# Batched matrix product in float16: all stores behind the loads, two groups' outputs in the input buffers

## Chip, core and metric

One core of a Trainium2 chip runs the whole problem. The metric is the device time of one execution in microseconds; of the kernel before, 4 runs are shown, with a median of 134.69 us (134.59 to 134.77). Engines are named as the profile names them: PE (matrix engine), DVE (vector engine), ACT (scalar engine), SP (here it only issues transfers).

## What is computed

For 32 batches, a 256 x 512 matrix times a 512 x 384 matrix, all float32 in memory:

```python
# x: (32, 256, 512), y: (32, 512, 384), out: (32, 256, 384)
return np.einsum('bij,bjk->bik', x, y).astype(np.float32)
```

Inputs are 16.78 MB of x and 25.17 MB of y, the output is 12.58 MB: 54.5 MB pass between memory and the core.

## The kernel before

The 32 batches are cut into 8 groups of 4 (N = 8, Q = 4). Each group takes a slot of 32 partitions for each of its 4 batches, so that four matrix products run in four row strips of PE side by side. What is done to a group n is written in the code as steps of one letter and the group's number, and the string PLAN fixes the order in which the steps are given out:

- x n (line 87) and y n (line 96): the loads, 2.10 MB and 3.15 MB, issued on SP. There are two buffers for x and two for y. A load waits until the group that used its buffer two groups earlier has been read by DVE.
- T n: DVE rounds x to float16 (line 106, one instruction of 128 x 4096) and transposes it in 32 x 32 blocks (line 113).
- R n: DVE rounds y to float16 in four parts (line 119).
- M n (line 132): 128 matmuls of 32 rows by 384 columns. The 8 banks of PSUM are named (e, g), e for the half of the output rows (0, 1) and g for the batch (0 to 3). PE first does the 64 matmuls of e = 0, with the depth index outside and g inside, so that all four banks of the half are filled at the same time and finish together; then the 64 of e = 1.
- C n and D n (line 153): the copies from PSUM to the output tile, C on ACT and D on DVE. There is one set of 8 banks, so the matmuls of the next group into a bank wait for the copies out of it.
- S n (line 160): the store of the group, 1.57 MB, issued on SP.

All steps are held in this order on each engine's own queue. SP is a queue like the others: a store or load that waits holds back what SP issues after it. Transfers are spread over 16 DMA engines.

WIDE_GROUPS (6 before) chooses between two layouts of the output. In a group below it, a copy takes 32 partitions of a bank (4 copies a bank); the bank (1, 3) is copied by DVE (4 copies) and the other 7 by ACT (28 copies); a partition of the output tile holds 8 output rows of one batch, stored as one run of 12 KB. In a group from it on, a copy takes 64 partitions (2 copies a bank) and a partition holds two runs of 6 KB. In group 6 before, ACT copies all 8 banks (16 copies); in group 7, ACT has the banks with even g and DVE those with odd g (8 copies each).

The output tiles come from a pool of 5 buffers: the output of group 5 takes the buffer of group 0's, and so on, and its first copy waits until the earlier store has landed.

The PLAN before:

```python
PLAN = """
x0 x1 y0
T0 x2 y1
T1 R0 M0 C0 x3 y2
T2 D0 R1 M1 C1 x4 y3
T3 D1 R2 M2 C2 x5 y4
T4 D2 R3 M3 C3 x6 y5
T5 D3 R4 M4 C4 x7 S0 S1 S2 y6
T6 D4 R5 M5 C5 y7
T7 D5 R6 M6 C6 R7 M7 C7 D7 S3 S4 S5 S6 S7
"""
```

Of the kernel before, what the change touches and what calls it, by code (L numbers as in the profile page):

```python
# [1 line left out]

# [4 lines left out]


MM_DT = mybir.dt.float16
F32 = mybir.dt.float32  # L10
P = 128


Q = 4
STEP = 4
O_BUFS = 5
WIDE_GROUPS = 6

# [5 lines that stand above are left out]
T2 D0 R1 M1 C1 x4 y3  # L26
T3 D1 R2 M2 C2 x5 y4
T4 D2 R3 M3 C3 x6 y5
T5 D3 R4 M4 C4 x7 S0 S1 S2 y6
T6 D4 R5 M5 C5 y7  # L30
T7 D5 R6 M6 C6 R7 M7 C7 D7 S3 S4 S5 S6 S7
"""


@with_exitstack
def kernel(
    ctx: ExitStack,
    tc: tile.TileContext,
    x: bass.AP,
    y: bass.AP,  # L40
    out: bass.AP,
):
    nc = tc.nc

    B, I, J = x.shape
    _, _, K = y.shape

    PQ = P // Q
    R = I // PQ
    T = J // PQ  # L50
    TW = T // 2
    NE = I // P
    N = B // Q

    x_pool = ctx.enter_context(tc.tile_pool(name="x_pool", bufs=2))
    y_pool = ctx.enter_context(tc.tile_pool(name="y_pool", bufs=2))
    xr_pool = ctx.enter_context(tc.tile_pool(name="xr_pool", bufs=1))
    xt_pool = ctx.enter_context(tc.tile_pool(name="xt_pool", bufs=3))
    yr_pool = ctx.enter_context(tc.tile_pool(name="yr_pool", bufs=2))
    o_pool = ctx.enter_context(tc.tile_pool(name="o_pool", bufs=O_BUFS))  # L60
    psum_pool = ctx.enter_context(
        tc.tile_pool(name="psum", bufs=1, space=bass.MemoryType.PSUM)
    )

    keep = tc.keep_in_program_order

    bank = {
        (e, g): psum_pool.tile([P, K], F32, name=f"o_ps_{e}_{g}") for e in range(NE) for g in range(Q)
    }

    x_of, y_of, xt_of, yr_of, ps_of, o_of = {}, {}, {}, {}, {}, {}

    def width(n):
        return PQ if n < WIDE_GROUPS else 2 * PQ

    def on_vector(n, e, g):
        if n < WIDE_GROUPS:  # L80
            return (e, g) == (NE - 1, Q - 1)
        return n == N - 1 and g % 2 == 1

    def load_x(n):
        x_of[n] = x_pool.tile([P, R, J], F32, name="x_sb")
        keep(
            nc.sync.dma_start(
                out=x_of[n],
                in_=x[n * Q : (n + 1) * Q].rearrange("g (p r) j -> (g p) r j", r=R),
            )  # L90
        )

    def load_y(n):
        y_of[n] = y_pool.tile([P, T, K], F32, name="y_sb")
        keep(
            nc.sync.dma_start(
                out=y_of[n],
                in_=y[n * Q : (n + 1) * Q].rearrange("g (q t) k -> (g q) t k", t=T),
            )
        )  # L100

    def transpose_x(n):


        x_r = xr_pool.tile([P, R, J], MM_DT, name="x_r")
        keep(nc.vector.tensor_copy(x_r, x_of.pop(n)))  # L106
        xt_of[n] = xt_pool.tile([P, NE, TW, P], F32, name="xt_sb")
        b = width(n) // PQ
        src = x_r.bitcast(F32).rearrange("p (b h e) (q t) -> p b e t h q", b=b, e=NE, t=TW)
        dst = xt_of[n].rearrange("p e t (h s b) -> p b e t h s", s=PQ, b=b)  # L110
        for e in range(NE):
            for c in range(b):
                keep(nc.vector.transpose(dst[:, c, e], src[:, c, e]))  # L113

    def round_y(n):
        y_sb = y_of.pop(n)
        yr_of[n] = yr_pool.tile([P, T, K], MM_DT, name="y_r")
        for a in range(0, T, STEP):
            keep(nc.vector.tensor_copy(yr_of[n][:, a : a + STEP], y_sb[:, a : a + STEP]))  # L119

    def multiply(n):
        xt = xt_of.pop(n).bitcast(MM_DT).rearrange("p e t (m c) -> p e t m c", c=2)
        y_r = yr_of.pop(n)
        o_of[n] = o_pool.tile([P, R, K], F32, name="o_sb")
        for e in range(NE):
            for g in range(Q):
                ps_of[n, e, g] = bank[e, g]
            for t in range(T):
                for g in range(Q):
                    s = slice(g * PQ, (g + 1) * PQ)  # L130
                    keep(
                        nc.tensor.matmul(  # L132
                            ps_of[n, e, g],
                            xt[s, e, t // 2, :, t % 2],
                            y_r[s, t],
                            start=(t == 0),
                            stop=(t == T - 1),
                        )
                    )

    def collect(n, vector):
        w = width(n)
        per = P // w
        copy = nc.vector.tensor_copy if vector else nc.scalar.copy
        o = o_of[n].rearrange("p (u f) k -> p u f k", u=Q // per)
        for e in range(NE):
            for g in range(Q):
                if on_vector(n, e, g) != vector:
                    continue
                ps = ps_of.pop((n, e, g))  # L150
                a = g % per * w
                for h in range(per):
                    keep(copy(o[a : a + w, g // per, h * NE + e], ps[h * w : (h + 1) * w]))  # L153

    def store(n):
        w = width(n)
        per = P // w
        dst = out[n * Q : (n + 1) * Q].rearrange("(u g) (s f) k -> (g s) u f k", g=per, s=w)
        keep(
            nc.sync.dma_start(  # L160
                out=dst, in_=o_of.pop(n).rearrange("p (u f) k -> p u f k", u=Q // per)
            )
        )

    parts = {
        "x": load_x,
        "y": load_y,
        "T": transpose_x,
        "R": round_y,
        "M": multiply,  # L170
        "C": lambda n: collect(n, False),
        "D": lambda n: collect(n, True),
        "S": store,
    }
    for step in PLAN.split():
        parts[step[0]](int(step[1:]))


# [1 line left out]
_INS = ['x', 'y']  # L180
_OUTS = [((32, 256, 384), 'float32')]


# [23 lines left out]
```

## Time and profile before

| what | value |
|---|---|
| median of 4 runs | 134.69 us |
| profiled execution: device time | 135.1 us |
| its span, first to last instruction | 133.2 us |
| read and written | 41.94 MB, 12.58 MB |
| mean rate over the span | 410 GB/s |
| share of the span in which packets of the transfers' queue are under way | 96.9% of 16 engines |
| busy: DVE, ACT, PE | 96.0, 91.7, 58.3 us |

Times of instructions are microseconds from the start of the span. In a row of the timeline the columns are start, duration from the first to the last instruction of the run, engine, line, operation, output<-input with the form, the count, and in brackets the idle time of the engine just before with what ended it. "SPq" is the queue that issues transfers. The lines by tenths show the span in 40 slices of 3.33 us. PEclk is the share of the full clock that PE was granted.

### The profile page before, as it was taken

How to read it: one execution, taken by the hardware profiler on the slowest of the kernel's cores; microseconds unless marked ns; L12 is line 12 of the kernel's file. 1: busy time of each engine (PE TensorE's matmuls, PEld its weight loads, DVE VectorE, ACT ScalarE, POOL GpSimd, SP SyncE). 2: the span in 40 equal slices, each digit the busy share in tenths (PEclk: the TensorE clock that was granted, in tenths of full speed). 3: DMA queues.
4: the chain of work that ended last, by engine and by line, in shares of the span. 5: the costliest groups of instructions: out<-in, count | busy, mean ns of one | idle time of the engine just before them, and what ended most of it. 6: DMA issues, size and time to landing. Idle time of an engine off the chain costs nothing.

```text
span 133.2 us, 2437 instructions
## 1 busy us (share of the span) xinstructions
PE 58.3 (44%) x1024; PEld 32.7 (25%) x1024; DVE 96.0 (72%) x92; ACT 91.7 (69%) x193; POOL 0.2 (0%) x4
## 2 busy tenths in 40 slices
PE   0000003991396139623953295419540079676000
PEld 0000002560144014411531153205320045344000
DVE  0039999699969999999996999599951090766300
ACT  3000000079999999999999999999999975997200
POOL 0000000000000000000000000000000000000000
PEclk9999999999779986998699959995999559999955
DMA  5999999999999999999999999999999999999992
GB/s 118 408 443 445 428 416 438 455 421 408 443 440 435 398 450 408 428 423 448 435 401 440 421 460 389 412 424 432 450 407 450 435 413 376 433 424 415 413 417 116
DMA packets 3723, 54.68 MB, mean 410 GB/s; under 512 B 384, under 2 KB 384, under 8 KB 896
## 3 DMA queue, kind: packets, MB, share of 16 engines
q1 hardware_dynamic: 3712, 54.53, 96.9%
q8 instruction: 8, 0.13, 0.4%
q14 instruction: 3, 0.02, 0.0%
HBM read 41.94 MB, written 12.58 MB: 409 GB/s over the span
## 4 chain that ended last, share of the span: by engine, by line
ACT 35%; DMA 28%; DVE 16%; PE 10%; issue 4%; DVEq 1%
ACT o_sb L153 35%; DMA y_sb<-in_y_dram 22%; PE o_ps L132 10%; DMA x_sb<-in_x_dram 6%; DVE xt_sb L113 6%; DVE y_r L119 4%; DVE x_r L106 3%; DVE o_sb L153 3%; DVEq L202 1%
## 5 line engine op out<-in xcount | busy, mean ns | idle before, releaser
L153 ACT COPY o_sb<-o_ps 32x384 f32<-32x384 f32 (+1 forms) x192 | 90.4, 471 | 31.6 <-PE o_ps L132 26.2
L132 PE MATMUL o_ps<-y_r,xt_sb 32*128 32x384 f16 x1024 | 58.3, 382 | 63.8 <-DVE y_r L119 52.7
L132 PEld LDWEIGHTS <-xt_sb 32*128 32x128 f16 x1024 | 32.7, 109 | 89.1 <-DVE y_r L119 33.2
L119 DVE CAST y_r<-y_sb 128x1536 f16<-128x1536 f32 x32 | 28.5, 953 | 10.1 <-DMA y_sb<-in_y_dram 9.9
L113 DVE STREAM_TRANSPOSE xt_sb<-x_r 128x1024 f32<-128x1024 f32 (+1 forms) x20 | 31.7, 1632 | 0.3
L106 DVE CAST x_r<-x_sb 128x4096 f16<-128x4096 f32 x8 | 18.3, 2291 | 11.3 <-DMA x_sb<-in_x_dram 11.2
L153 DVE COPY o_sb<-o_ps 32x384 f32<-32x384 f32 (+1 forms) x32 | 17.8, 556 | 6.7 <-PE o_ps L132 3.9
L153 ACT ACT_TABLE_LOAD x1 | 1.3, 1283 | 0.7 <-PEq L191 0.7
L191 POOL MEMSET const-bfloat16-1.0<- 128x1 bf16 x1 | 0.1, 102 | 0.0
L191 POOL MEMSET const-uint8-127<- 128x1 uint8 x1 | 0.1, 102 | 0.0
L191 POOL MEMSET const-float32-0.0<- 128x1 f32 x1 | 0.1, 99 | 0.2 <-issue 0.2
L191 POOL MEMSET const-float32-1.0<- 128x1 f32 x1 | 0.1, 99 | 0.0
## 6 DMA issues: line engine op xcount, KB each, us to landing
y_sb<-in_y_dram SPq DMA_DIRECT2D x8, 3072.0 KB, 21.1
x_sb<-in_x_dram SPq DMA_DIRECT2D x8, 2048.0 KB, 21.9
out_dram<-o_sb SPq DMA_DIRECT2D x8, 1536.0 KB, 25.6
```

Of the source, the lines that this page charges most:

```text
L106: keep(nc.vector.tensor_copy(x_r, x_of.pop(n)))
L113: keep(nc.vector.transpose(dst[:, c, e], src[:, c, e]))
L119: keep(nc.vector.tensor_copy(yr_of[n][:, a : a + STEP], y_sb[:, a : a + STEP]))
L132: nc.tensor.matmul(ps_of[n, e, g], xt[s, e, t // 2, :, t % 2], y_r[s, t], start=(t == 0), stop=(t == T - 1),)
L153: keep(copy(o[a : a + w, g // per, h * NE + e], ps[h * w : (h + 1) * w]))
L191: nc = _bacc.Bacc("TRN2", target_bir_lowering=False, num_devices=1)
L202: with _tile.TileContext(nc) as tc:
```

## The change

WIDE_GROUPS becomes 7, so that group 6 is copied and stored as groups 0 to 5 are. The stores S0, S1 and S2 move from ahead of y6 to behind y7, so that on SP every store stands behind every load. The output tiles of groups 5 and 6 are taken from the pool of the x tiles (the first 3072 of a partition's 4096 elements), since x6 and x7 are the last to use these two buffers; the output of group 7 then takes the buffer that group 0's had. D6 is a step of its own now, on DVE behind R7.

```diff
-WIDE_GROUPS = 6
+WIDE_GROUPS = 7
+
+O_IN_X = (5, 6)
...
-T5 D3 R4 M4 C4 x7 S0 S1 S2 y6
-T6 D4 R5 M5 C5 y7
-T7 D5 R6 M6 C6 R7 M7 C7 D7 S3 S4 S5 S6 S7
+T5 D3 R4 M4 C4 x7 y6
+T6 D4 R5 M5 C5 y7 S0 S1 S2 S3 S4
+T7 D5 R6 M6 C6 R7 D6 M7 C7 D7 S5 S6 S7
...
     def multiply(n):
...
-        o_of[n] = o_pool.tile([P, R, K], F32, name="o_sb")
+        if n in O_IN_X:
+            x_sb = x_pool.tile([P, R, J], F32, name="x_sb")
+            o_of[n] = x_sb.rearrange("p r j -> p (r j)")[:, : R * K].rearrange(
+                "p (r k) -> p r k", r=R
+            )
+        else:
+            o_of[n] = o_pool.tile([P, R, K], F32, name="o_sb")
```

## The prediction

> **What bounds the kernel now.** I read the page's lines by tenths first, then the transfer queue's waits, then the timeline of ACT, PE, DVE and SP from 98 us on.
>
> ```profile
> ACT  3000000079999999999999999999999975997200
> DMA  5999999999999999999999999999999999999992
> ```
>
> The 16 transfer engines are full from the second slice to the last but one: the queue carries 54.5 MB without a hole, and ends the kernel. ACT, too, is full from slice 9 on.
>
> ```profile
> SPq L202 <- DMA out_dram<-o_sb: 7.3, 2, 3.7
> DMA to landing us min/median/max: 7.9/25.6/30.7
> ```
>
> The first line (the transfer queue's own waits) is the end of the program: it waits for S6 and then, 3.7 us longer, for S7. The second (issue to landing of the eight stores) has S7 as its minimum, 7.9 us. S7 moves 1.57 MB, which take 3.7 us; so it stood behind S6 in a full queue. Issued at 124.50, it landed at 132.4, and the span ended 0.8 us later at 133.2.
>
> How late could S7 have been issued? The trace records a landing for each of the 16 transfer engines. They don't run level: S6 was done on the first engine at 126.06 and on the last at 128.74, S7 at 129.74 and 132.4. On the first engine S7 needed 129.74 - 124.50 = 5.24 us, 1.5 us more than its 3.7 us of data. So the last engine left S7 about 132.4 - 129.7 = 2.7 us of slack. The question is how much later S7 is issued after the change.
>
> ```profile
> 27.50 81.49 ACT L153 COPY o_sb<-o_ps 32x384 f32<-32x384 f32 x168 [25.49 <-PE o_ps L132]
> 111.52 9.80 ACT L153 COPY o_sb<-o_ps 64x384 f32<-64x384 f32 x20 [2.53 <-issue]
> ```
>
> ACT's timeline: 168 copies, groups 0 to 5, without a pause from 27.50 to 108.99: 81.49/168 = 0.485 us each. Then 2.53 us idle, because y6 came late, then the wide copies of group 6 (16) and the first of group 7.
>
> ```profile
> 77.00 29.27 DMA y_sb<-in_y_dram
> 106.28 3.56 DVE L119 CAST y_r<-y_sb 128x1536 f16<-128x1536 f32 x4 [5.68 <-DMA y_sb<-in_y_dram]
> ```
>
> Chain and DVE timeline: y6, issued at 77.00, lands at 106.26, since S0 to S2 were ahead of it; DVE waits.
>
> ```profile
> 119.39 5.49 SPq L160 DMA_DIRECT2D out_dram<-o_sb  x2
> 119.41 2.75 PE L132 MATMUL o_ps<-y_r,xt_sb 32*128 32x384 f16 x61 [0.66 <-ACT o_sb L153]
> 122.17 2.27 DVE L153 COPY o_sb<-o_ps 64x384 f32<-64x384 f32 x4 [1.28 <-PE o_ps L132]
> ```
>
> The end before: ACT's last copy of group 6 (119.36) lets S6 go and frees the last bank; PE does the second half of group 7 in 2.75 us; DVE copies its two banks in 2.27 us to 124.44; S7 is issued.
>
> **The change part by part.**
>
> *Stores behind loads.* Up to x7 (issued at 66.0) nothing differs. y6 waits for R4 and goes at 77.00 as before, but without three stores ahead (3 x 3.7 = 11 us) it lands near 95.3. y7 waits for R5, which ends at 90.55; 4.7 us of queue are still left then, so the queue stays full. y7 lands near 95.3 + 7.4 = 102.7 (3.15 MB at the page's 426 GB/s) instead of 114.0. S0 to S3 are issued right behind it at 91 to 93, S4 when C4 ends at 95.4: 5 x 3.7 = 18.5 us of work, to 121. S5 waits for C5 at 109.0, well ahead of that, and reaches to 124.7. SP has nothing but stores behind these waits, so no load is held back. The queue moves the same bytes, and by itself would again end near 132.4. Gain of this part: R6 can start when D5 ends (100.6) and R7 right after (104.2 to 107.7), so ACT's pause of 2.53 us goes. It does not reach the queue's end.
>
> *Outputs in x buffers.* No instruction more. x6's and x7's buffers are read for the last time by DVE's rounding, which ends at 79.2 and 92.8; C5 and C6 write them from 95.4 and 109.0: waits already over, cost 0. Group 7's output needs S0 landed (about 106.4) and is first written at about 119: 0. Without that cover it would be the store's landing time.
>
> *Group 6 narrow.* This is the price. ACT gets 28 copies instead of 16; a copy takes the same whichever form (470 ns against 474 ns in the groups by form). DVE's 4 copies for D6 (2.3 us) lie in its idle time after R7. In the transfer, 256 runs of 12 KB replace 512 of 6 KB: the trace's packets took 463 ns against 235, so 8 x 463 instead of 16 x 235 ns on an engine, 0.05 us less. T6's two large transposes for four small save 0.1 us beside ACT: nothing.
>
> The path through the end:
> - C5 ends at 108.99, as before (ACT has had no pause since 27.50, and M5 comes before it as now).
> - C6: 28 x 0.485 = 13.58, to 122.57. S6 goes then, 3.2 us later than before.
> - M7's second half needs the last bank from C6: 2.77 us, to 125.38. Its first half needs the bank freed after 16 copies, 108.99 + 7.76 = 116.75, and is done by 121.2 even at the slow pace below.
> - D7's last four copies: 2.27 us, to 127.65. ACT's last four end before. S7 is issued at 127.7, against 124.50: 3.2 us later.
> - S7's slack was 2.7 us. So at least 3.2 - 2.7 = 0.5 us is lost: with 5.24 us from issue to landing, S7 lands at 132.95.
>
> *The price of a store into a drained queue* is not in this trace; S7 of before never met an empty one. From below: nothing, if issue to landing takes up to 4.7 us, because then the queue's own end at 132.4 decides. From above: the only transfer into an empty queue is x0.
>
> ```profile
> 0.73 8.06 DMA x_sb<-in_x_dram
> 0.00:2.00 2.00, 0.00 (x0) 0.00 (x0) 0.00 (x0) 1.27 (x1) 0.20 (x4) 1.00 0.54 106
> 2.00:4.00 2.00, 0.00 (x0) 0.00 (x0) 0.00 (x0) 0.01 (x1) 0.00 (x0) 1.00 0.59 205
> 4.00:6.00 2.00, 0.00 (x0) 0.00 (x0) 0.00 (x0) 0.00 (x0) 0.00 (x0) 1.00 0.99 426
> ```
>
> First the chain, then the table by stretches, whose last column is GB/s: 8.06 us for 2.10 MB that take 4.9 at 426 GB/s, so 3.1 us of start; with that S7 lands at 127.7 + 3.1 + 3.7 = 134.5. The first transfer of a program is a poor likeness of its last store; S7's own 5.24 us is the nearest row. I take 5.5: 0.25 more for engines that do not start level. S7 lands at 133.2, 0.8 later than before.
>
> The Trainium skill, "DMA: Bandwidth & Descriptors", section on the anatomy of one DMA, gives a fit of about 2.0 us fixed (mostly the wait for the write's receipt) plus bytes/436 GB/s, made on the software path. By it S7 would need 5.6 us and land at 133.3; this fixed part, which a full queue hides, is what speaks against the change.
>
> *PE's clock.* In these two rows of the table by stretches, the same number of matmuls:
>
> ```profile
> 62.50:65.70 3.20, 3.20 (x44) 1.82 (x47) 3.17 (x3) 3.12 (x7) 0.00 (x0) 0.50 1.03 443
> 68.30:71.00 2.70, 2.70 (x62) 1.76 (x61) 1.66 (x1) 2.63 (x6) 0.00 (x0) 1.00 1.00 425
> ```
>
> The column before the last two is the granted clock: after a pause PE has 0.50 (44 matmuls in 3.2 us), later 1.00 (62 in 2.7). At half clock M7's second half takes about 62 x 3.2/44 = 4.5 us, 1.7 us more on the path. After the change PE pauses from about 111.8 to 116.75, so M7's first half is likely slow (to 121.2, hidden behind C6). The second follows 1.4 us later; in five groups it was at 1.00 in that place, so I cost it at 2.77.
>
> The Trainium skill, "TensorE: Matmul & The Clock Gate", Part 1, says that an idle window of about 3.4 us halves the clock and a busy one restores it. By it the second half runs at full clock, unless the windows fall so that the busy one counts for too little; the sum would then be 1.7 us higher.
>
> **Sum.** +3.2 (S7's issue) - 2.7 (slack) + 0.25 (start) = +0.75, rounded to +0.8: span 133.2 + 0.8 = 134.0. The profiled execution before took 135.1 for this span, so it would take 135.9; the median of the runs lies 0.4 below the profiled one, at 134.69, so the forecast for the median is 135.5.
>
> **Rivals.** 0.2% (0.27 us) is about what a measurement of this kernel tells from no change.
> - *The forecast*, S7 into a drained queue, 0.3 to 1.4 us lost: 135.0 to 136.1. For: the sum above, whose first four steps are rows of before. Chance 0.62.
> - *The queue still ends last.* If a store from issue to landing takes 4.7 us or less, the queue's 132.4 stands: 134.7. For: on the first engine S7 followed S6 without a pause, so 5.24 is an upper bound there. Against: 3.7 is data, and only 1.0 is left for start and receipt. Within 0.2%: chance 0.13.
> - *Slower by more*: x0's start (3.1 us instead of 1.8), 136.8, or M7's second half at half clock, 137.1. Chance 0.20 for over 136.1.
> - *Faster: changes of direction cost the queue time.* Before there are three between loads and stores, after it one. For: y7 came 7.8 us after y6 (106.26 to 114.07), where 426 GB/s make 7.4. Two fewer at 0.4 us would end the queue at 131.6, 133.9 in all. But S7 must then land before 132.16, so issue to landing must take under 4.45 us, 0.7 more than its data, or ACT must copy faster than in any stretch of before. With what such a landing leaves, 134.3. Chance 0.05.
>
> That the change doesn't do what it says is excluded by the order of SP's queue: 16 loads, then 8 stores.
>
> Faster 0.05, same 0.13, slower 0.82. The range goes from 134.7, the queue's own end, to 136.8, x0's start: what lies below and the half clock hold under 2 in 10.
>
> **What would show it.** Right: ACT without a pause from 27.5 to about 122.6; y6 landing near 95, y7 near 103; S7 issued near 127.7; the transfers' tenths dropping below 9 in the slices around 126 to 130. Wrong: S7 issued before 127, PE's last 60 matmuls over 4 us, or full tenths up to a landing at 132.4.

## The result, and the profile after

The changed kernel takes 135.23 us (median of 47 runs, 134.21 to 135.94) against 134.48 us before (69 runs, 134.18 to 135.02): a ratio of 1.0046, 95% interval 1.0035 to 1.0057, slower by half a per cent. The profiled execution took 135.7 us with a span of 133.9 us; before it was 135.1 and 133.2. The runs after the change spread over 1.7 us, those before over 0.8. The forecast was 0.8 us slower, against 0.75 between the medians and 0.6 by the ratio; it gave the sign and the size, and said nothing of the spread.

The lines by tenths of the page after:

```profile
ACT  3000000089999999999999999999999999999500
DMA  5999999999999999999999999999999999999883
```

ACT's pause in slices 33 and 34 is gone: it has 8 in slice 9 and 9 in every slice from 10 to 37. The transfer engines have tenths of 8, 8 and 3 at the end, where they had 9, 9 and 2.

The transfer queue's waits for the last two stores at the end of the program (S7 from the output pool, S6 from an x buffer), and the issue to landing of the stores from either:

```profile
SPq L210 <- DMA out_dram<-o_sb: 3.6, 1, 3.6
SPq L210 <- DMA out_dram<-x_sb: 1.7, 1, 1.7
```

```profile
DMA to landing us min/median/max: 5.9/17.4/25.9
```

S7 (from the output pool) still lands 3.6 us after S6 (from an x buffer), but S7 now needs 5.9 us from issue instead of 7.9. The queue no longer had work for it to stand behind: that is shown by one row of the table by stretches (the last two columns are the share of the 16 transfer engines and GB/s), with the stretches around it:

```profile
124.00:126.00 2.00, 0.83 (x21) 0.35 (x10) 1.16 (x3) 1.26 (x3) 0.00 (x0) 1.00 0.98 412
126.00:128.00 2.00, 0.00 (x0) 0.00 (x0) 1.07 (x2) 0.63 (x2) 0.00 (x0) 1.00 0.48 203
128.00:130.00 2.00, 0.00 (x0) 0.00 (x0) 0.00 (x0) 0.00 (x0) 0.00 (x0) 1.00 1.02 418
```

Half of the queue's capacity is lost between 126 and 128 us, where before it moved 427 GB/s:

```profile
126.00:128.00 2.00, 0.00 (x0) 0.00 (x0) 0.00 (x0) 0.00 (x0) 0.00 (x0) 0.80 1.02 427
```

S6 met engines that had nothing left, too: S5 was done on the first engine at 122.32, and S6, issued at 122.03, only at 126.92. The forecast had S7 alone in a drained queue.

The rows of ACT's timeline, and then those of PE, DVE and SP near the end (the last row is that of before):

```profile
27.09 67.79 ACT L161 COPY o_sb<-o_ps 32x384 f32<-32x384 f32 x140 [25.09 <-PE o_ps L140]
94.91 27.10 ACT L161 COPY x_sb<-o_ps 32x384 f32<-32x384 f32 x56
122.03 1.93 ACT L161 COPY o_sb<-o_ps 64x384 f32<-64x384 f32 x4
```

```profile
116.24 4.46 PE L140 MATMUL o_ps<-y_r,xt_sb 32*128 32x384 f16 x63 [1.61 <-ACT x_sb L161]
122.05 2.78 PE L140 MATMUL o_ps<-y_r,xt_sb 32*128 32x384 f16 x62 [1.35 <-ACT x_sb L161]
```

```profile
124.82 2.27 DVE L161 COPY o_sb<-o_ps 64x384 f32<-64x384 f32 x4 [1.89 <-PE o_ps L140]
```

```profile
127.14 0.38 SPq L168 DMA_DIRECT2D out_dram<-o_sb  x1
```

```profile
124.50 0.38 SPq L160 DMA_DIRECT2D out_dram<-o_sb  x1
```

This is the forecast chain, link by link: 196 narrow copies on ACT without a pause from 27.09 to 122.01, 2.78 us of matmuls in group 7's second half, 2.27 us of copies on DVE, S7 issued at 127.14 (124.50 before). The first half of group 7 ran at the slow pace (4.46 us for 63 matmuls), hidden behind ACT.

### The profile page after: what moved, and what is told of

Its sections match the earlier page's. It is cut to its first block, busy times and chain, and to the rows that moved or that the text cites. A ratio compares the mean times of both kernels' runs of the same rounds, so it can differ in the third digit from the quotient of the medians.

```text
span 133.9 us, 2448 instructions
## 1 busy us (share of the span) xinstructions
PE 60.3 (45%) x1024; PEld 34.3 (26%) x1024; DVE 98.1 (73%) x94; ACT 97.1 (72%) x205; POOL 0.2 (0%) x4
## 4 chain that ended last, share of the span: by engine, by line
ACT 65%; DVE 11%; PE 9%; DMA 6%; issue 3%; DVEq 0%; ACTq 0%
ACT o_sb L161 49%; ACT x_sb L161 16%; PE o_ps L140 9%; DVE xt_sb L115 6%; DMA x_sb<-in_x_dram 6%; DVE x_r L108 3%; DVE o_sb L161 1%; DVE y_r L121 1%; DVEq L210 0%; ACTq L161 0%
## 5 line engine op out<-in xcount | busy, mean ns | idle before, releaser
L161 ACT COPY o_sb<-o_ps 32x384 f32<-32x384 f32 (+1 forms) x148 | 69.5, 470 | 28.0 <-PE o_ps L140 25.8
L140 PE MATMUL o_ps<-y_r,xt_sb 32*128 32x384 f16 x1024 | 60.3, 390 | 64.5 <-DVE y_r L121 46.6
L140 PEld LDWEIGHTS <-xt_sb 32*128 32x128 f16 x1024 | 34.3, 111 | 90.1 <-issue 34.0
L161 ACT COPY x_sb<-o_ps 32x384 f32<-32x384 f32 x56 | 26.3, 469 | 0.8
L161 DVE COPY o_sb<-o_ps 32x384 f32<-32x384 f32 (+1 forms) x28 | 15.6, 556 | 11.6 <-ACT x_sb L161 7.1
L161 DVE COPY x_sb<-o_ps 32x384 f32<-32x384 f32 x8 | 4.4, 555 | 5.7 <-PE o_ps L140 5.6
```

What stands on the lines that cost most here:

```text
L140: nc.tensor.matmul(ps_of[n, e, g], xt[s, e, t // 2, :, t % 2], y_r[s, t], start=(t == 0), stop=(t == T - 1),)
```

## Experiments

Theory A, from the prediction: the 12 more copies that ACT makes in group 6 push S7 past the slack that a full queue gave it. Theory B: the new order of the stores or the new place of two outputs costs the time. Ratios are to the kernel before, run on the same chip.

### Group 6 wide again

```diff
-WIDE_GROUPS = 7
+WIDE_GROUPS = 6
```

> The changed kernel with group 6 in the wide form again (16 copies, all on ACT, none on DVE), all else as changed: stores behind loads, outputs 5 and 6 in the x buffers. Theory A (the 12 more ACT copies of group 6 push S7 past the slack that the queue leaves): C6 ends near 108.4 + 16 x 0.485 = 116.2, the second half of group 7's matmuls near 119, S7 is issued near 121.4, under 125, so the queue's own end decides again: S7 lands near 132.4, span near 133.2, ratio to before 1.000 within 0.002. Theory B (the order of the stores, or the x buffers as targets, cost the time): span near 133.9, ratio near 1.005 as for the change.

Measured: ratio 0.9999 (0.9991 to 1.0008), 11 runs from 134.31 to 134.55. The rows of ACT (its row of 44 copies is group 5's 28 and group 6's 16) and the issue to landing of its stores:

```profile
94.40 21.39 ACT L161 COPY x_sb<-o_ps 32x384 f32<-32x384 f32 x44
115.82 1.93 ACT L161 COPY o_sb<-o_ps 64x384 f32<-64x384 f32 x4
```

```profile
120.93 0.38 SPq L168 DMA_DIRECT2D out_dram<-o_sb  x1
```

```profile
DMA to landing us min/median/max: 10.9/18.0/26.5
```

S7 is issued at 120.93 and waits 10.9 us in a full queue. So stores behind loads, and outputs in x buffers, cost the end nothing; theory B falls. All of the loss came with the narrow form of group 6. The spread is smaller as well: 0.24 us over these 11 runs.

### The narrow form alone, in the kernel before

```diff
-WIDE_GROUPS = 6
+WIDE_GROUPS = 7
...
-T7 D5 R6 M6 C6 R7 M7 C7 D7 S3 S4 S5 S6 S7
+T7 D5 R6 M6 C6 R7 D6 M7 C7 D7 S3 S4 S5 S6 S7
```

> The kernel before with only group 6 in the narrow form (28 copies on ACT, 4 on DVE behind R7); stores and buffers as before. Theory A: y6 still lands near 106.3, C6 starts near 111.5 and ends near 111.5 + 13.6 = 125.1, group 7's second half near 127.9, DVE's last copy near 130.2; S7 then needs 5.9 us into a drained queue, landing near 136.1: span near 136.9, 3.7 us over before (ratio near 1.027). Theory B (the narrow form costs nothing by itself): ratio near 1.000, or 1.005 if 12 KB runs are what costs.

Measured: ratio 1.0335 (1.0310 to 1.0359), 4 runs from 138.45 to 139.47, span of the profile 137.2. Two lines of its ACT and its stores:

```profile
111.57 15.49 ACT L153 COPY o_sb<-o_ps 32x384 f32<-32x384 f32 x32 [3.99 <-issue]
```

```profile
DMA to landing us min/median/max: 6.1/26.0/31.7
```

ACT pauses 3.99 us for y6, which the stores ahead of it held back, and resumes at 111.57, as reckoned; S7 goes at 130.25 and takes 6.1 us. The span was expected at 136.9. The ratio came out higher than 1.027 mostly because I set it against the span 133.2 of before's first profile, which is 0.6 us over its usual 132.6. So the earlier loads of the change are worth most of the narrow form's price: without them it costs 4.5 us (138.89 against 134.38), with them 0.75.

### DVE takes more of group 6: one bank, then two

```diff
         if n < WIDE_GROUPS:
-            return (e, g) == (NE - 1, Q - 1)
+            return g == Q - 1 and (n == N - 2 or e == NE - 1)
```

> The changed kernel, but in group 6 DVE also copies the bank (0, 3), so that ACT has 24 copies there and DVE 8; stores, buffers and 12 KB runs as changed. Theory A: C6 on ACT ends 4 x 0.485 = 1.9 us earlier, near 120.1, S7 is issued near 125.2 and needs 5.9 us: 131.1, under the queue's end of 132.4, which decides: span near 133.2, ratio to before 1.000 within 0.002. Theory B (order of stores, x buffers or the 12 KB form): ratio near 1.005.

Measured with 24 copies on ACT: ratio 1.0020 (1.0000 to 1.0039), 11 runs from 134.24 to 135.53. The profiled run has a span of 132.5 and S7 issued at 125.23 as expected:

```profile
125.23 0.38 SPq L168 DMA_DIRECT2D out_dram<-o_sb  x1
DMA to landing us min/median/max: 6.5/17.4/25.9
```

The first engine needed 5.03 us for S7, as in an empty queue; on the last, S7 still stood behind S6 (landed there at 128.06 and 131.72). Two of the other runs took 135.5; they have no profile that would show why. The ratio lies on the edge of what theory A gave it. With two more banks on DVE than in the change:

```diff
-            return (e, g) == (NE - 1, Q - 1)
+            return (e, g) in ((0, 3), (1, 2), (1, 3)) if n == N - 2 else (e, g) == (NE - 1, Q - 1)
```

> The changed kernel, but in group 6 DVE copies the banks (0, 3), (1, 2) and (1, 3), so that ACT has 20 copies there and DVE 12; all else as changed. Theory A: C6 ends on ACT near 108.4 + 20 x 0.485 = 118.1, S7 is issued near 123.3, 1.7 us ahead of the latest time that the queue's end allows (near 126): ratio to before 1.000 within 0.001, and, since runs in which ACT starts up to 1 us later are still covered, all runs within 0.5 us of each other, as with 16 copies (134.31 to 134.55) and unlike with 24 (134.24 to 135.53). Theory B (12 KB runs or the x buffers cost something that the wide form hid): ratio 1.002 or more.

Measured with 20 copies: ratio 0.9985 (0.9969 to 1.0001), 12 runs from 134.13 to 134.72. S7 goes at 123.41 and waits 8.2 us:

```profile
123.41 0.39 SPq L168 DMA_DIRECT2D out_dram<-o_sb  x1
DMA to landing us min/median/max: 8.2/17.6/26.0
```

The runs lie within 0.59 us, a little over the 0.5 expected. With the result of 28 copies (the change, 1.0046) and of 16 (group 6 wide, 0.9999) this is a dose and its answer: 28, 24 and 20 narrow copies on ACT give 1.0046, 1.0020 and 0.9985, and below 20 nothing more is gained. The 12 KB runs themselves cost nothing: with 20 copies they are still there.

### Warming PE ahead of group 0

If ACT has no pause from its first copy to its last, whatever makes the first copy late must show at the end. 120 matmuls on data of group 0 were put ahead of its own, in the time in which PE waits for y0.

```diff
+WARM = 120
...
+        for i in range(WARM if n == 0 else 0):
+            s = slice(i % Q * PQ, (i % Q + 1) * PQ)
+            keep(
+                nc.tensor.matmul(
+                    bank[0, i % Q], xt[s, 0, 0, :, 0], xt[s, 0, 0:3, :, 0], start=True, stop=True
+                )
+            )
```

> The changed kernel with 120 matmuls more on PE ahead of group 0's, on x of group 0 alone, in the time in which PE waits for y0; their results are overwritten by the real ones. Theory A with the clock of PE as the source of the spread (the changed kernel's 47 runs lie from 134.21 to 135.94, the 69 of before from 134.18 to 135.02): ACT is without a pause from group 0's first copy to the end, so the end moves with that copy. With PE at full clock the first 64 matmuls take under 4 us instead of 5.3, ACT starts near 25.5 to 26 instead of 27.1, and S7 is issued 1.1 us or so earlier, near 126: lands near 132, under or at the queue's end; ratio near 1.000, runs within 134.2 to 135.0. Theory C (the spread comes from the clock in group 7's second half, or from memory): ACT starts earlier, but the runs stay spread over more than 1.2 us and the ratio over 1.003.

Measured: ratio 1.0158 (1.0121 to 1.0194), 6 runs from 135.49 to 137.19: a clear miss. ACT's timeline and DVE's in that kernel:

```profile
25.42 13.56 ACT L169 COPY o_sb<-o_ps 32x384 f32<-32x384 f32 x28 [23.41 <-PE o_ps L148]
41.91 54.32 ACT L169 COPY o_sb<-o_ps 32x384 f32<-32x384 f32 x112 [2.92 <-PE o_ps L148]
```

```profile
26.99 2.29 DVE L109 CAST x_r<-x_sb 128x4096 f16<-128x4096 f32 x1 [2.47 <-DMA x_sb<-in_x_dram]
```

The first copy did come at 25.42. But then ACT waited 2.92 us for group 1: x2 landed at 26.90 instead of 25.48 (in the changed kernel), DVE waited for it, and group 1's matmuls began late and at the slow pace. The landing records put the delay on one transfer engine: 15 were done by 25.6. In the same trace a 16 KB packet of an instruction queue ran at 21.3 for 1.06 us; in the changed kernel the first such packet comes at 30.4. That the extra instructions drew it forward fits both traces; it was not tested apart. What this run does show is that a delay of 1.3 us at 42 us (41.91 against 40.66) is still there at the end: the span is 135.3, 1.4 us over the changed kernel's.

### The changed kernel twice more

No edit; two more profiles to see where its spread comes from.

> The changed kernel itself, once more, for a second profile. Theory (the spread of its runs is the start of ACT's chain, moved by the landing of the first loads and by where PE's slow stretch falls in group 0 and 1): the time over 134.4 follows ACT's last pause: span = (end of the last pause of ACT, 27.1 in the first profile) + 106.8 within 0.3 us, but not under 132.4; the second half of group 7's matmuls takes 2.8 us as in the first profile. Rival (PE at half clock in the second half of group 7): that piece takes 4 to 5 us in a slow run, with ACT's start unchanged.

> The same as the run before it, for a third profile: span = end of ACT's last pause + 106.8 within 0.3 us, but not under 132.4, if the spread comes from the start of ACT's chain; a piece of 4 to 5 us in the second half of group 7's matmuls if it comes from there.

Measured: 134.68 us with a span of 132.8, and 135.59 us with 133.8. Their rows of group 0's matmuls and ACT's first rows (the first run, then the second):

```profile
21.91 6.96 PE L140 MATMUL o_ps<-y_r,xt_sb 32*128 32x384 f16 x128 [21.91 <-DVE y_r L121]
```

```profile
26.29 67.94 ACT L161 COPY o_sb<-o_ps 32x384 f32<-32x384 f32 x140 [24.28 <-PE o_ps L140]
```

```profile
21.86 7.83 PE L140 MATMUL o_ps<-y_r,xt_sb 32*128 32x384 f16 x128 [21.86 <-DVE y_r L121]
```

```profile
27.11 67.94 ACT L161 COPY o_sb<-o_ps 32x384 f32<-32x384 f32 x140 [25.10 <-PE o_ps L140]
```

PE begins group 0 within 0.1 us of the same time in both, but its 128 matmuls take 6.96 or 7.83 us (8.27 in the first profile), and ACT starts at 26.29 or 27.11. The second half of group 7 takes 2.77 and 2.84 us, at full pace in both, so the rival falls. Spans reckoned from ACT's start were 133.1 and 133.9; both hold within 0.3 us.

The trace's records of the granted clock say where the difference arises. Their first entry, at 1.00, comes 3.26 and 5.03 us after PE's first matmul in these two profiles and 5.92 us after it in the first one, the order of the times for the 128 matmuls: 6.96, 7.83 and 8.27 us.

### Extra matmuls ahead of groups 0, 1 and 2

```diff
+WARM = {0: (28, 4), 1: (28, 2), 2: (32, 2)}
...
+        for i in range(WARM.get(n, (0, 1))[0]):
+            ahead = xt_of[n + 1].bitcast(MM_DT).rearrange("p e t (m c) -> p e t m c", c=2)
+            w = i % WARM[n][1]
+            s = slice(w * PQ, (w + 1) * PQ)
+            keep(
+                nc.tensor.matmul(
+                    bank[0, w],
+                    ahead[s, 0, 0, :, 0],
+                    ahead[s, 0, 0:3, :, 0],
...
```

> The changed kernel with 28, 28 and 32 extra matmuls on PE ahead of those of groups 0, 1 and 2, on x of the next group, timed to run in the 2 to 4 us just before y arrives; their results are overwritten. It follows on the run with 120 extra matmuls ahead of group 0, where ACT did start at 25.4 but then waited 2.9 us for group 1, whose x landed later and whose matmuls ran at half clock. Theory (the spread of the changed kernel and about half of its loss are the start of ACT's chain, set by PE's clock in groups 0 to 2): ACT's last pause ends at 26.3 or before in every run, S7 is issued at 126.5 or before, time 134.3 to 134.9 in all runs, median under 134.8, ratio 1.000 to 1.002. Rival (the spread comes from the landing of loads or from the end): runs still spread from 134.3 to 135.9, ratio 1.003 to 1.006; if the extra matmuls delay a group, over that.

Measured: ratio 1.0003 (0.9991 to 1.0016), median 134.43, 11 runs from 134.19 to 134.99. ACT's first rows and the last store:

```profile
25.18 13.54 ACT L175 COPY o_sb<-o_ps 32x384 f32<-32x384 f32 x28 [23.17 <-PE o_ps L154]
39.94 54.29 ACT L175 COPY o_sb<-o_ps 32x384 f32<-32x384 f32 x112 [1.23 <-PE o_ps L154]
```

```profile
126.49 0.39 SPq L182 DMA_DIRECT2D out_dram<-o_sb  x1
```

88 matmuls that compute nothing, all before 48 us, take back the loss at 133 us and about half of the spread: 0.80 us against 1.73. The fastest and the slowest run lie 0.1 us outside the 134.3 to 134.9 that were expected. In all four profiles S7 is issued a nearly fixed time (100.05 to 100.33 us) after ACT's last pause:

| profile | PE's first matmul to ACT's first copy | end of ACT's last pause | S7 issued | between | span |
|---|---|---|---|---|---|
| changed kernel, first | 5.31 | 27.09 | 127.14 | 100.05 | 133.9 |
| again, first | 4.38 | 26.29 | 126.56 | 100.27 | 132.8 |
| again, second | 5.25 | 27.11 | 127.44 | 100.33 | 133.8 |
| extra matmuls | 3.45 | 39.94, less group 0's 13.57: 26.37 | 126.49 | 100.12 | 132.5 |

### The outputs of groups 5 and 6 back in their own pool

```diff
-O_IN_X = (5, 6)
+O_IN_X = ()
```

> The changed kernel with the outputs of groups 5 and 6 in the pool of output tiles again: group 5's output then takes group 0's buffer and waits for S0, which stands behind y7. Theory A (the wait for a buffer goes straight into ACT's chain, which has no slack left): C5 starts when S0 lands, near 106.2, instead of 94.9: 11.3 us later; everything behind it moves by that, S7 issued near 138.4, span near 145, time near 147 (ratio near 1.09). Rival (ACT catches up in the pauses that PE leaves): ratio under 1.05.

Measured (one run): 146.47 us, span 144.7.

```profile
106.07 29.11 ACT L161 COPY o_sb<-o_ps 32x384 f32<-32x384 f32 x60 [11.39 <-DMA out_dram<-o_sb]
```

The wait for S0 is 11.39 us (11.3 expected), and the span is 144.7 - 133.9 = 10.8 us longer: nearly all of it reaches the end. So it is the x buffers that spare the new order of the stores this wait.

### Both remedies

The extra matmuls, and DVE's three banks of group 6, in one kernel.

> Both remedies at once: the extra matmuls ahead of groups 0 to 2, and DVE copying the banks (0, 3), (1, 2) and (1, 3) of group 6. S7 is then issued near 122.5, about 3.5 us ahead of the latest time that the queue allows. Theory (the queue's 54.5 MB are the floor; the changed kernel only lost its cover over it): no gain over one remedy alone, ratio 0.998 to 1.001, all runs within 0.6 us. Rival (something of the computation still shows at the end): a ratio of 0.996 or less.

Measured: median 134.23 us, ratio 0.9983 (0.9971 to 0.9995), 11 runs from 134.13 to 134.38. S7 goes at 122.96 and waits 8.7 us in a full queue. Its median is the lowest of all, 0.17% ahead of the kernel before, but not apart from the version with 20 copies (0.9985), and it is as steady as group 6 wide (runs within 0.25 and 0.24 us). That 12 KB runs save 0.05 us of it was reckoned; where the rest of 0.2 us comes from was not tested. No remedy takes the end below the queue's.

## Why the prediction was right

- *Bound now and after.* Right. The queue's end was the limit, with slack for S7; removing ACT's pause changed nothing while that held (group 6 wide: 0.9999).
- *Stores behind loads.* Right: y6 and y7 landed at 95.28 and 102.56 (95.3 and 102.7 forecast), S4 at 120.76 (121), S5 at 124.40 (124.7).
- *Outputs in x buffers cost 0.* Right, shown by the wide form; the price without that cover, 10.8 us, by the run with its own pool.
- *Group 6 narrow.* Right: from the end of ACT's last pause to S7 the sum made 127.7 - 27.50 = 100.2 us; four profiles gave 100.05 to 100.33. S7 was issued at 127.14 and not at 127.7 mostly because ACT began at 27.09 in this profile and at 27.50 in that of before.
- *Luck in the numbers.* The profile of before that I reckoned from was late in two places. ACT began at 27.50, against 26.22 to 27.11 in the eight later profiles without extra matmuls, and the last engine was 2.67 us behind the first, against 1.8 to 2.3 in the later profiles while their queues were full. The first made the reckoned S7 0.4 to 1.3 us late by these profiles, the second the queue's end, and with it the slack, 0.4 to 0.9 us, so that most of both fell out of the difference. In the profile after, too, two errors offset each other: S7 was issued 0.56 us earlier than forecast and took 0.45 us longer than the 5.5 to land (133.09 against 133.2).
- *Price of a store into a drained queue.* I took 5.5 us between 4.7 and 6.8, and the size was well placed: S7 took 5.9, 5.4 and 5.5 us in three profiles of the changed kernel, 6.1 in the narrow form alone, 5.5 in the run with its own pool, 5.9 with 120 extra matmuls and 5.2 with 88. x0's start (6.8) was too much. My reason for the 0.25 us over the 5.24 of the first engine, that the engines do not start level, holds for one engine only. In all seven profiles fifteen of the sixteen engines were done 5.19 to 5.20 us after S7's issue (the first after 5.03 to 5.05), and only the last took 5.21 to 6.13. In six of them a 16 KB instruction packet ran between S6's issue and its landing (in the first profile at 123.1, for 1.88 us; there 15 engines had landed by 132.34 and the last at 133.09), and the last landings of S6 and S7 lie 3.6 us apart, as in a full queue. In the seventh, with 88 extra matmuls, there was no such packet, and the last engine needed 5.21. That the packet makes the difference fits all seven; no run has tested it apart.

The Trainium skill, "DMA: Bandwidth & Descriptors", in its section on the anatomy of one DMA, has 2.0 us plus bytes/436 GB/s, which makes an estimate of 5.6 us; seven profiles of drained queues gave 5.2 to 6.1, so the estimate holds here within about half a microsecond, for stores issued on SP and not on the software path that the section is about.

- *PE's clock.* Right where I looked: the second half of group 7 was at full pace in every profile. The step that was missing is earlier. I took ACT's start, 27.50, as fixed, since it was a row of before and nothing ahead of it is changed. But it moves from run to run with the time that PE needs for the first 64 matmuls (4.38 to 5.31 us), and the queue that used to hide this no longer does. Three profiles of the changed kernel and the run with 88 extra matmuls, which shortened this time to 3.45 us, show that as a source of the spread, around a median close to the forecast. The 47 runs fit it: the mean granted clock of a run marks the pattern in which the clock's stretches fell (in the profile with 0.897 stretches of 10.2 us at 1.00 and 3.4 us at 0.50 take turns, in the two with 0.80 stretches of 6.8 us of each), and the 16 runs with 0.800 or less took 134.21 to 135.22 us, the 12 with 0.87 or more 135.32 to 135.93. How much of the spread it makes is not shown, since only three runs of this kernel have a trace.

The Trainium skill, "TensorE: Matmul & The Clock Gate", Part 1, says that the window of about 3.4 us runs freely and that the moment of the change therefore varies by 500 ns either way, with where in the window the first matmul falls. That the moment varies agrees with these starts (5.31, 4.38 and 5.25 us for the same work), but by more than that: the clock's record begins 3.26 to 5.92 us after the first matmul.

- *The rivals.* The queue's own end decided where enough copies were taken off ACT (S7 waited 8.2 us with 20 copies, 10.9 with 16). With PE warmed by 88 matmuls it did not: S7 took 5.2 us, as in a drained queue, but was issued early enough to land at 131.70. Changes of direction between loads and stores gave nothing: with one instead of three, the wide form had 0.9999. The row that I gave for them, y7 7.8 us after y6, holds none, as both are loads and follow each other.

## What to carry to other kernels

Here a transfer queue that was full to the end hid delays ahead of it up to the slack of its last store: issued at 120.93 or 123.41, S7 cost nothing, at 127.14 about 0.75 us. Before work is added to an engine that feeds the last store, measure that slack (issue to landing, less what the store needs alone; here 7.9 - 5.2 = 2.7 us) and compare it with the work. When the slack is used up, not only the mean moves: a start that varies by 1 us from run to run, unseen before, shows in the spread. Work that was moved earlier helps only if the engine behind it can use it: the loads moved ahead here made the narrow form 3.8 us cheaper (4.5 against 0.75), but the fastest version is only 0.17% below the kernel before.

## What had not been expected of the hardware

- The granted clock reads 1.00 in the stretch of the first matmuls, though in the first profile of the changed kernel 40 of them took 3.0 us, against 62 in 2.8 us later. The trace's records of the clock begin only at 27.70. In this stretch the pace tells more than the column:

```profile
21.80:24.80 3.00, 3.00 (x40) 1.72 (x43) 2.53 (x3) 0.00 (x0) 0.00 (x0) 1.00 1.08 464
```

- The program's own instructions come through the same transfer engines: eight or nine packets of 16 KB, each of about 0.9 to 2 us. Each makes one engine late, and what is behind on it stays behind while the queue is full. In the changed kernel the sixteen landings of a load lie within 0.53 us up to x2; after the packet at 30.4 one of them is more than 1.5 us behind the first, after that at 44.2 two, and after those at 58.0, 71.9, 85.3 and 99.3 three, four, five and six. Over all profiles the landings of one transfer lie 0.5 to 1.1 us apart at the start and 1.8 to 2.7 us before the end, and a full queue ends with its latest engine (S7 of before: 129.74 on the first, 132.4 on the last). In the run with 120 extra matmuls a landing 1.4 us late came with such a packet.
